# The scale and shift of two modulated norms as columns on transposed rows, in a two-block transformer kernel

## The chip, the cores and the metric

The kernel runs on one core of one Trainium2 chip as one program. The metric is device microseconds. The engines are TensorE (PE: matmuls and transposes into PSUM; PEld are its weight loads), VectorE (DVE), ScalarE (ACT) and GpSimd (POOL), with SyncE (SP) issuing most DMAs. Each engine works its own instructions in order and waits on semaphores for the others.

## The reference, cut to what matters

The input is x [1, 512, 2048] in float32. The first block is attention beside a state space mixer, an output projection and a LayerNorm. The second block modulates two RMS norms with six vectors from c:

```python
def rms_norm(x, g):
    return x * lax.rsqrt(jnp.mean(x * x, axis=-1, keepdims=True) + 1e-6) * g

h = first_block(x, ...)                  # ends in _layer_norm(ALPHA * h + mixed @ w_out, ln_g, ln_b)
shift1, scale1, gate1, shift2, scale2, gate2 = jnp.split(mod, 6, axis=-1)
u = rms_norm(h, norm1_g) * (1.0 + scale1) + shift1          # first modulated norm
u_a, v_a, q, k, v = jnp.split(u @ w_in, SPLIT_POINTS, axis=-1)
q, k = rms_norm(per head q, q_norm_g), rms_norm(per head k, k_norm_g)
y = concat(spatial_gating(u_a, v_a, gm_norm_g, gm_ws, gm_bs), stick_breaking_attention(q, k, v))
x = h + gate1 * (rms_norm(per group of 128 y, out_norm_g) @ w_out_2)
m = rms_norm(x, norm2_g) * (1.0 + scale2) + shift2          # second modulated norm
# top-1 of 4 expert groups, top-2 of its 8 experts (SwiGLU, 32 experts of width 256)
out = x + gate2 * moe(m)
```

## The kernel before, in words

Tokens lie in four tiles of 128 rows. A float32 product is made of three matmuls (L148 to L150) on a high and a low part of each operand. `wchunk` makes the parts of the weights: SP loads a raw chunk of 128x1024 (L136, four buffers), ACT casts the high part `wh` (L123, 1.05 us), DVE subtracts it for the low part `wl` (L124), three buffers each. `split_into` makes the two parts of an operand in the same lines, as pieces `op` of 128x256. PE's operands need the model dimension on the partitions, so rows are transposed by PE in blocks of four 128x128 tiles (L203) into a PSUM tile `s`.

*Norms* (`phase_b`, `norms`). The projection `w_out` runs for tokens 0 and 1 and then for 2 and 3. After each half, LayerNorm (L780, L781) and the first modulated norm follow token by token: DVE multiplies by the root `rs` and the broadcast row `g1` (L788), POOL adds the broadcast row `s1` (L789), and `rows_to_op` (L715) transposes and splits into `self.opt`. The four rows `lng`, `lnb`, `g1`, `s1` are 1 MB broadcasts that SP loads. While PE works at one half, DVE, POOL and ACT prepare the other.

*Mixer* (`mixer2`). The projections `w_in_2` read `self.opt`, again by halves for q and k. `head_norm` takes ACT squares of 128x128 (L798), a Newton root on DVE (L192 to L197) and a DVE multiply into a row tile (L803), which PE transposes. The mask multiply of the gating weights (`ws`, L854) is a DVE instruction there.

*Route* (`route`). `w_out_2` runs by halves. Per block of 512 columns DVE makes the residual `r` (L956, L957), POOL starts the second norm (L958: r times the row `gs`, which L926 and L927 make), ACT squares, PE transposes for the router's logits. After a half, ACT (L986) and POOL (L987), or DVE alone (L984), apply root and shift row `sh`, and ACT's queue writes `h2` to HBM (L988). DVE then works out the routing (L999 and on) with one ACT exponential (L1010). The router's own columns `col` are loaded element by element (L889 to L891).

*Gather and experts.* POOL's indirect DMAs fetch 8 tiles of 128 gathered rows of `h2` (L1136), PE transposes them in blocks, ACT (L1149, even blocks) and DVE (L1145, odd blocks) evacuate them into `xg`; for the first tile the other engine copies a window for expert 0 (L1147, L1151). 32 experts follow with 1 MB weight loads.

The order on each engine is fixed when the program is built, by a scheduler that follows the code's order and `issue_after` hints.

Of the kernel before, what the change touches and what calls it, by code (L numbers as in the profile page):

```python
# [103 lines left out]
class Kern:  # L104
# [622 lines left out]
    def phase_b(self):  # L727
# [3 lines left out]
        self.x1 = self.dram.tile([512, 2048], F32, name='x1')  # L731
        with tc.tile_pool(name='ln', **kw) as ln:
            t = [ln.tile([128, 2048], F32, name=n) for n in ('lng', 'lnb', 'g1', 's1')]
            lng, lnb, g1, s1 = t
            st = ln.tile([128, 4, 4, 6], F32, name='st')

            def load(k):

                if k < 2:
                    nc.sync.dma_start(r[:, k, :], a['x'][k])  # L740
                elif k < 6:
                    src = (a['norm1_g'], self.mod[:, 2048:4096], a['ln_g'], a['ln_b'])[k - 2]
                    nc.sync.dma_start((g1, s1, lng, lnb)[k - 2], src.broadcast_to([128, 2048]))
                    if k == 3:
                        nc.vector.scalar_tensor_tensor(g1, s1, 1.0, g1, OP.add, OP.mult)
                elif k == 6:
                    nc.sync.dma_start(s1, self.mod[:, 0:2048].broadcast_to([128, 2048]))
                else:
                    for i in (2, 3):
                        nc.sync.dma_start(r[:, i, :], a['x'][i])  # L750

            for half in ((0, 1), (2, 3)):
# [10 lines left out]
                for i in half:  # L763
                    self.norms(ln, i, st[:, i], lng, lnb, g1, s1)
        with tc.tile_pool(name='rt', **kw) as self.rt:
            with tc.tile_pool(name='b2', **kw) as b2:
                self.mixer2(b2, self.opt)
            with tc.tile_pool(name='m0', **kw) as self.m0:
                self.route()

    def norms(self, ln, i, st, lng, lnb, g1, s1):
# [14 lines left out]
        for b in range(4):  # L786
            c = slice(b * 512, b * 512 + 512)
            nc.vector.scalar_tensor_tensor(t[:, c], r[:, i, c], rs, g1[:, c], OP.mult, OP.mult)  # L788
            nc.gpsimd.tensor_tensor(t[:, c], t[:, c], s1[:, c], OP.add)  # L789
            self.rows_to_op(t[:, c], self.opt[2 * b:2 * b + 2], i)  # L790

    def head_norm(self, pool, x, g, out, scale=1.0 / 128, eps=1e-6):
# [8 lines left out]
        for h in range(4):  # L801
            c = slice(h * 128, h * 128 + 128)
            nc.vector.scalar_tensor_tensor(out[:, c], x[:, c], rs[:, h:h + 1], g[h], OP.mult, OP.mult)  # L803

    def mixer2(self, b2, op):
        tc, nc, a, r = self.tc, self.nc, self.a, self.r
        kw = dict(bufs=1, side='right', reuse_waits='tile')
        gq = self.row_bcast(b2, a['q_norm_g'], 128, 'gq')
        gk = self.row_bcast(b2, a['k_norm_g'], 128, 'gk')
# [16 lines left out]
        with tc.tile_pool(name='sb', **kw) as sb:  # L826
            for b, g, half in ((0, gq, (0, 1)), (1, gk, (0, 1)), (0, gq, (2, 3)), (1, gk, (2, 3))):
                ps = self.gemm('R', a['w_in_2'][b], op, bg=1, toks=half)
                xT = qk[b]
                for i in half:  # L830
                    t = b2.tile([128, 512], F32, tag='row', name='row', bufs=3)
                    self.head_norm(b2, ps[i], [g] * 4, t)
# [21 lines left out]
            nc.vector.tensor_tensor(ws, ws, self.mask_le[:, None, :].to_broadcast([128, 4, 128]), OP.mult)  # L854
            ps = self.gemm('R', a['w_in_2'][3], op)
            for i in range(4):
                t = b2.tile([128, 512], F32, tag='row', name='row', bufs=3)
                vn = b2.tile([128, 512], F32, tag='row', name='vn', bufs=3)
                nc.scalar.activation(t, ps[i], AF.Gelu)
                self.head_norm(b2, t, [gm[:, h * 128:(h + 1) * 128] for h in range(4)], vn)  # L860
# [10 lines left out]
            for i in range(4):  # L871
                t = b2.tile([128, 512], F32, tag='row', name='row', bufs=3)
                self.head_norm(b2, o[:, i, :], [go[:, 512 + h * 128:512 + (h + 1) * 128] for h in range(4)], t)
                self.rows_to_op(t, opy[0:2], i)
            for i in range(4):
                t = b2.tile([128, 512], F32, tag='row', name='row', bufs=3)
                vn = b2.tile([128, 512], F32, tag='row', name='vn', bufs=3)
                nc.scalar.activation(t, ps[i], AF.Gelu)  # L878
                nc.vector.tensor_tensor(t, t, sg[:, i, :], OP.mult)
                self.head_norm(b2, t, [go[:, h * 128:(h + 1) * 128] for h in range(4)], vn)  # L880
# [4 lines left out]
    def router(self):  # L885

        nc, a, xr = self.nc, self.a, self.rt
        col = xr.tile([128, 3, KT], F32, name='col')
# [16 lines left out]
    def route(self):  # L905
# [35 lines left out]
        for half in ((0, 1), (2, 3)):  # L941
# [5 lines left out]
            for b in range(4):  # L947
# [5 lines left out]
                for i in half:  # L953
# [4 lines left out]
                    nc.gpsimd.tensor_tensor(h2[i % 2][:, c], r[:, i, c], gs[:, c], OP.mult)  # L958
# [173 lines left out]
    def gather(self, s):  # L1132
# [319 lines left out]
```

## Time and profile before

| what | value |
|---|---|
| median of 3 runs | 2021.39 us (2020.11 to 2024.66) |
| profiled execution | 2020.36 us, span 2018.5 us, mean granted clock 0.973 |
| PE busy | 1909.2 us, 95% of the span |
| DVE, ACT, POOL busy | 1217.5, 862.8, 325.9 us |
| HBM traffic | 479.76 MB read, 37.84 MB written |

Times in the trace count from the start of the span. The first block's mixers run to about 838 us, the norms and `w_out` to 1070, the mixer of the second block to about 1330, route to 1445, the gather to 1500, the experts to the end. An idle time in brackets stands before the instruction that ended it, with what released it. The granted clock is that of TensorE, as a share of 2.4 GHz; 0.50 is the level of 1.2 GHz.

### The profile page before, as it was taken

How to read it: one execution, taken by the hardware profiler on the slowest of the kernel's cores; microseconds unless marked ns; L12 is line 12 of the kernel's file. 1: busy time of each engine (PE TensorE's matmuls, PEld its weight loads, DVE VectorE, ACT ScalarE, POOL GpSimd, SP SyncE). 2: the span in 40 equal slices, each digit the busy share in tenths (PEclk: the TensorE clock that was granted, in tenths of full speed). 3: DMA queues.
4: the chain of work that ended last, by engine and by line, in shares of the span. 5: the costliest groups of instructions: out<-in, count | busy, mean ns of one | idle time of the engine just before them, and what ended most of it. 6: DMA issues, size and time to landing. Idle time of an engine off the chain costs nothing. (4 is left out here: it accounts for less than half of the span.)

```text
span 2018.5 us, 30419 instructions
## 1 busy us (share of the span) xinstructions
PE 1909.2 (95%) x11830; PEld 1232.9 (61%) x11830; DVE 1217.5 (60%) x2210; ACT 862.8 (43%) x1426; POOL 325.9 (16%) x251
## 2 busy tenths in 40 slices
PE   8999999999999999999997999889589999999996
PEld 5677776666777778887876888778442333333331
DVE  4778975444677796558796664877633434333433
ACT  3343223335443453434444554644234444444453
POOL 0422133000011110001111120043331111111111
PEclk9999999999999999999998999989699999999998
DMA  8654664545665674586654332656699999999994
GB/s 305 224 188 166 232 230 169 181 179 204 239 218 199 213 258 136 183 311 235 197 200 144 116 116 96 248 199 219 260 346 358 399 400 399 401 403 396 401 416 183
DMA packets 115493, 502.85 MB, mean 249 GB/s; under 512 B 22299, under 2 KB 23835, under 8 KB 84499
## 3 DMA queue, kind: packets, MB, share of 16 engines
q1 hardware_dynamic: 108642, 479.81, 64.0%
q0 software_dynamic: 6080, 16.83, 3.2%
q10 hardware_dynamic: 624, 4.24, 0.5%
q8 instruction: 94, 1.54, 0.3%
q14 instruction: 53, 0.43, 0.1%
HBM read 479.76 MB, written 37.84 MB: 256 GB/s over the span
## 5 line engine op out<-in xcount | busy, mean ns | idle before, releaser
L124 DVE TENSOR_TENSOR wl<-raw,wh 128x1024 fp32r<-128x1024 f32 (+1 forms) x272 | 357.8, 1320 | 224.4 <-ACT wh L123 223.5
L123 ACT CAST wh<-raw 128x1024 fp32r<-128x1024 f32 (+1 forms) x272 | 280.5, 1031 | 445.9 <-PE g L150 200.7
L149 PE MATMUL g<-wl,op 128*128 128x512 f32 (+1 forms) x896 | 351.0, 392 | 5.6 <-DVE wl L124 5.5
L150 PE MATMUL g<-wh,op 128*128 128x512 f32 (+1 forms) x896 | 348.3, 389 | 0.0
L148 PE MATMUL g<-wh,op 128*128 128x512 f32 (+1 forms) x896 | 333.7, 393 | 2.1 <-ACT row L878 1.0
L148 PE MATMUL g<-op,wh 128*128 128x512 f32 x672 | 272.0, 406 | 4.4 <-ACT z L404 3.0
L149 PE MATMUL g<-op,wh 128*128 128x512 f32 x672 | 268.1, 400 | 0.0
L150 PE MATMUL g<-op,wl 128*128 128x512 f32 x672 | 262.2, 396 | 0.0
L1178 PE MATMUL s<-wop,x 128*32 128x512 f32 x1710 | 251.4, 593 | 0.0
L1180 PE MATMUL s<-wop,x 128*32 128x512 f32 x570 | 251.0, 593 | 0.0
L148 PEld LDWEIGHTS g<-wh,op 128*128 128x128 f32 x896 | 171.2, 191 | 42.8 <-issue 6.6
L149 PEld LDWEIGHTS g<-wl,op 128*128 128x128 f32 x896 | 171.0, 191 | 41.6 <-DVE wl L124 8.5
L150 PEld LDWEIGHTS g<-wh,op 128*128 128x128 f32 x896 | 170.8, 191 | 33.4 <-issue 1.1
L1178 PEld LDWEIGHTS s<-wop,x 128*32 128x32 f32 x1710 | 68.2, 110 | 158.2 <-issue 154.0
L148 PEld LDWEIGHTS g<-op,wh 128*128 128x128 f32 x672 | 127.6, 190 | 52.9 <-issue 19.7
L150 PEld LDWEIGHTS g<-op,wl 128*128 128x128 f32 x672 | 127.3, 189 | 31.6 <-issue 3.9
L1188 ACT COPY yt<-g 32x512 f32<-32x512 f32 x192 | 111.3, 580 | 79.4 <-DVE y L1271 43.2
L149 PEld LDWEIGHTS g<-op,wh 128*128 128x128 f32 x672 | 127.9, 190 | 26.2 <-issue 1.4
L1178 PE MATMUL g<-wop,hT 128*32 128x512 f32 x810 | 120.7, 592 | 3.7 <-ACT hT L1227 2.2
L1189 DVE TENSOR_TENSOR gu<-gu,s 96x512 f32<-96x512 f32 x32 | 21.8, 682 | 169.5 <-ACT gu L1188 169.5
L1188 ACT COPY gu<-s 32x512 f32<-32x512 f32 x96 | 55.6, 579 | 159.1 <-PE s L1180 157.5
L1180 PE MATMUL g<-wop,hT 128*32 128x512 f32 x270 | 120.9, 594 | 0.0
(400 smaller groups left out, 2817.9 us busy)
## 6 DMA issues: line engine op xcount, KB each, us to landing
wop<-in_w_gu SPq DMA_DIRECT2D x95, 1024.0 KB
raw<-in_w_in SPq DMA_DIRECT2D x168, 512.0 KB
wm<-in_w_mod SPq DMA_DIRECT2D x96, 512.0 KB
raw<-in_w_mod SPq DMA_DIRECT2D x96, 512.0 KB
raw<-in_w_out SPq DMA_DIRECT2D x96, 512.0 KB
wop<-in_w_dn SPq DMA_DIRECT2D x45, 1024.0 KB
w<-in_w_gu SPq DMA_DIRECT2D x33, 1024.0 KB
w<-in_w_dn SPq DMA_DIRECT2D x19, 1024.0 KB
```

The lines of the kernel that those rows point to most:

```text
L123: nc.scalar.copy(hi, src)
L124: (lo_eng or nc.vector).tensor_tensor(lo, src, hi.bitcast(F32), OP.subtract)
L148: nc.tensor.matmul(out, lhsT=a[0], rhs=b[0], start=start, stop=False)
L149: nc.tensor.matmul(out, lhsT=a[0], rhs=b[1], start=False, stop=False)
L150: nc.tensor.matmul(out, lhsT=a[1], rhs=b[0], start=False, stop=stop)
L1178: nc.tensor.matmul(main[i][32 * s:32 * s + 32], lhsT=xs[i][:, 32 * s:32 * s + 32], rhs=w[i], start=first[i], stop=last[i], tile_position=( ...
L1180: self.mm = nc.tensor.matmul(ps[o][96:128], lhsT=xs[3][:, 32 * o:32 * o + 32], rhs=w[3], start=first[3], stop=last[3], tile_position=(0, 96))
L1188: self.last_copy = nc.scalar.copy(t[32 * s:32 * s + 32], ps[s][96:128])
L1189: nc.vector.tensor_tensor(t, t, main[0:W], OP.add)
```

## The change

In `norms`, ACT scales a row block by the root alone (Copy, scale `rs`); PE transposes it; ACT applies scale and bias columns to each 128x128 tile of the transposed block (Identity, 16 per token) into an SBUF tile `f` of two buffers, and the operand pieces are split from `f`. The columns `n1col` are loaded element by element (128 partitions x 16). In `route`, the rows `sh` and `gs` and all POOL work on `h2` go; `h2` becomes the residual times the root, by ACT (8 instructions of 128x512 per half). Scale and shift of the second norm are applied behind the gather: every 128x128 tile of a block gets the router's columns `col2`, by ACT Identity or DVE tensor_scalar, 64 each, and the first windows are copied from `xg` afterwards. The columns `col2` now lie in a pool that is open earlier. A new pool `hn`, opened before the norms' pool, holds the head norms' gains `gq` and `gk`, their sums and row tiles (all `head_norm` calls take it), so these no longer lie in the space that the norms use. The mask multiply of `ws` is put behind the last head norm of q and k.

```diff
@@ -729,22 +729,25 @@
...
+        hn_cm = tc.tile_pool(name='hn', bufs=1)
+        self.hn = hn_cm.__enter__()
...
-            t = [ln.tile([128, 2048], F32, name=n) for n in ('lng', 'lnb', 'g1', 's1')]
-            lng, lnb, g1, s1 = t
+            lng, lnb = [ln.tile([128, 2048], F32, name=n) for n in ('lng', 'lnb')]
...
+            col = ln.tile([128, 3, KT], F32, name='n1col')
...
             def load(k):
...
                 if k < 2:
                     nc.sync.dma_start(r[:, k, :], a['x'][k])
-                elif k < 6:
-                    src = (a['norm1_g'], self.mod[:, 2048:4096], a['ln_g'], a['ln_b'])[k - 2]
-                    nc.sync.dma_start((g1, s1, lng, lnb)[k - 2], src.broadcast_to([128, 2048]))
+                elif k < 5:
+                    src = (a['norm1_g'], self.mod[:, 2048:4096], self.mod[:, 0:2048])[k - 2]
+                    nc.sync.dma_start(col[:, k - 2, :], src.rearrange('o (k p) -> p (o k)', p=128))
                     if k == 3:
-                        nc.vector.scalar_tensor_tensor(g1, s1, 1.0, g1, OP.add, OP.mult)
-                elif k == 6:
-                    nc.sync.dma_start(s1, self.mod[:, 0:2048].broadcast_to([128, 2048]))
+                        nc.vector.scalar_tensor_tensor(col[:, 0, :], col[:, 1, :], 1.0, col[:, 0, :], OP.add, OP.mult)
+                elif k < 7:
+                    nc.sync.dma_start((lng, lnb)[k - 5], (a['ln_g'], a['ln_b'])[k - 5].broadcast_to([128, 2048]))
@@ -785,9 +789,16 @@
...
         for b in range(4):
             c = slice(b * 512, b * 512 + 512)
-            nc.vector.scalar_tensor_tensor(t[:, c], r[:, i, c], rs, g1[:, c], OP.mult, OP.mult)
-            nc.gpsimd.tensor_tensor(t[:, c], t[:, c], s1[:, c], OP.add)
-            self.rows_to_op(t[:, c], self.opt[2 * b:2 * b + 2], i)
+            nc.scalar.activation(t[:, c], r[:, i, c], AF.Copy, scale=rs)
+            pt = self.sps()
+            self.transposes(pt, [t[:, (4 * b + j) * 128:(4 * b + j + 1) * 128] for j in range(4)])
+            f = ln.tile([128, 512], F32, tag='f', name='f', bufs=2)
+            for j in range(4):
+                k, cj = 4 * b + j, slice(j * 128, j * 128 + 128)
+                nc.scalar.activation(f[:, cj], pt[:, cj], AF.Identity, scale=g1[:, k:k + 1], bias=s1[:, k:k + 1])
+            for u in range(2):
+                o, ts = self.opt[2 * b + u], slice(i * 128, i * 128 + 128)
+                self.split_into(o[0][:, :, ts], o[1][:, :, ts], f[:, u * 256:(u + 1) * 256].rearrange('p (k t) -> p k t', k=2))
...
@@ -851,13 +862,14 @@
...
-            nc.vector.tensor_tensor(ws, ws, self.mask_le[:, None, :].to_broadcast([128, 4, 128]), OP.mult)
+            with tc.issue_after(self.last_hn.ins):
+                nc.vector.tensor_tensor(ws, ws, self.mask_le[:, None, :].to_broadcast([128, 4, 128]), OP.mult)
@@ -885,7 +897,7 @@
...
-        col = xr.tile([128, 3, KT], F32, name='col')
+        col = self.col2 = self.xr.tile([128, 3, KT], F32, name='col')
@@ -919,13 +931,7 @@
...
-        sh = m0.tile([128, 2048], F32, name='sh')
         h2 = [m0.tile([128, 2048], F32, name='h2_%d' % i) for i in range(2)]
-        gs = self.row_bcast(m0, a['norm2_g'], 2048, 'g2')
-        nc.sync.dma_start(sh, self.mod[:, 8192:10240].broadcast_to([128, 2048]))
-        nc.gpsimd.tensor_tensor(sh, sh, gs, OP.mult)
-        nc.gpsimd.tensor_tensor(gs, sh, gs, OP.add)
-        nc.sync.dma_start(sh, self.mod[:, 6144:8192].broadcast_to([128, 2048]))
@@ -955,7 +961,6 @@
...
                     nc.vector.tensor_tensor(r[:, i, c], r[:, i, c], t, OP.add)
-                    nc.gpsimd.tensor_tensor(h2[i % 2][:, c], r[:, i, c], gs[:, c], OP.mult)
                     nc.scalar.activation(t, r[:, i, c], AF.Square, accum_out=ss[:, i, b:b + 1])
@@ -978,13 +983,7 @@
             for i in half:
                 for b in range(4):
                     c = slice(b * 512, b * 512 + 512)
-                    t = h2[i % 2][:, c]
-                    rs = r2[:, i - half[0]:i - half[0] + 1]
-                    if b >= 2:
-                        nc.vector.scalar_tensor_tensor(t, t, rs, sh[:, c], OP.mult, OP.add)
-                    else:
-                        nc.scalar.activation(t, t, AF.Copy, scale=rs)
-                        nc.gpsimd.tensor_tensor(t, t, sh[:, c], OP.add)
+                    nc.scalar.activation(h2[i % 2][:, c], r[:, i, c], AF.Copy, scale=r2[:, i - half[0]:i - half[0] + 1])
@@ -1138,17 +1137,19 @@
...
             pt = self.gps() if b % 2 else self.sps()
             self.transposes(pt, [t[:, (4 * b + j) * 128:(4 * b + j + 1) * 128] for j in range(4)])
-            k4 = slice(4 * b, 4 * b + 4)
-            src = pt.rearrange('p (k t) -> p k t', k=4)
-            dst = self.xg[:, k4, s * 128:(s + 1) * 128]
-            if b % 2:
-                nc.vector.tensor_copy(dst, src)
-                if s == 0:
-                    nc.scalar.copy(self.spread(self.win[0][:, k4, :]), src[:, :, 0:W].rearrange('p k (b a) -> p k b a', a=16))
-            else:
-                nc.scalar.copy(dst, src)
-                if s == 0:
-                    nc.vector.tensor_copy(self.spread(self.win[0][:, k4, :]), src[:, :, 0:W].rearrange('p k (b a) -> p k b a', a=16))
+            for j in range(4):
+                k = 4 * b + j
+                g, sh = self.col2[:, 0, k:k + 1], self.col2[:, 2, k:k + 1]
+                src, dst = pt[:, j * 128:j * 128 + 128], self.xg[:, k, s * 128:(s + 1) * 128]
+                if b % 2:
+                    nc.vector.tensor_scalar(dst, src, g, sh, OP.mult, OP.add)
+                else:
+                    nc.scalar.activation(dst, src, AF.Identity, scale=g, bias=sh)
+            if s == 0:
+                k4 = slice(4 * b, 4 * b + 4)
+                (nc.scalar.copy if b % 2 else nc.vector.tensor_copy)(
+                    self.spread(self.win[0][:, k4, :]), self.xg[:, k4, 0:W].rearrange('p k (b a) -> p k b a', a=16))
```

ACT around the norms of tokens 2 and 3, before (`hn_jk` are the head norms' squares, `op` operand pieces, `wh` weight casts):

```order
L123 CAST wh<-raw 128x1024 x5
L123 CAST op<-s 128x2x128 x4
L798 ACTIVATE hn_jk,hn_ss<-g 128x128 x3
L123 CAST op<-s 128x2x128
L798 ACTIVATE hn_jk,hn_ss<-g 128x128
L123 CAST op<-s 128x2x128
L798 ACTIVATE hn_jk,hn_ss<-g 128x128
L123 CAST op<-s 128x2x128
L798 ACTIVATE hn_jk,hn_ss<-g 128x128
L123 CAST op<-s 128x2x128
L798 ACTIVATE hn_jk,hn_ss<-g 128x128 x8
L835 COPY r<-s 128x4x128
```

and now, a stretch of the same place, with `f` the scaled and shifted blocks:

```order
L123 CAST wh<-raw 128x1024
L798 ACTIVATE f<-s,n1col 128x128 x4
L123 CAST wh<-raw 128x1024
L123 CAST op<-f 128x2x128 x4
L123 CAST wh<-raw 128x1024
L809 ACTIVATE hn_jk,hn_ss<-g 128x128
L798 ACTIVATE f<-s,n1col 128x128 x4
L123 CAST wh<-raw 128x1024
L809 ACTIVATE hn_jk,hn_ss<-g 128x128
L798 ACTIVATE f<-s,n1col 128x128 x4
L123 CAST op<-f 128x2x128 x2
L809 ACTIVATE hn_jk,hn_ss<-g 128x128
```

Squares of the head norms, Identity instructions, pieces and weight casts now alternate, where the squares stood behind the norms' pieces.

DVE at the head norms, before: the mask multiply L854 in the midst of two heads' roots, ahead of the first row (L803):

```order
L197 SCALAR_TENSOR_TENSOR rs_y<-rs_t,rs_y 128x4 x2
L195 TENSOR_TENSOR rs_t<-rs_y 128x4 x2
L196 SCALAR_TENSOR_TENSOR rs_t<-rs_t,hn_ss 128x4
L854 TENSOR_TENSOR ws<-ws,cst 128x512
L196 SCALAR_TENSOR_TENSOR rs_t<-rs_t,hn_ss 128x4
L197 SCALAR_TENSOR_TENSOR rs_y<-rs_t,rs_y 128x4 x2
L195 TENSOR_TENSOR rs_t<-rs_y 128x4
L803 SCALAR_TENSOR_TENSOR row<-g,rs_y,gq 128x128 x4
```

and now, at the last of the rows for q and k (L814; the first stands 110 rows earlier):

```order
L814 SCALAR_TENSOR_TENSOR row<-g,rs_y,gk 128x128 x4
L196 SCALAR_TENSOR_TENSOR rs_t<-rs_t,hn_ss 128x4
L197 SCALAR_TENSOR_TENSOR rs_y<-rs_t,rs_y 128x4
L195 TENSOR_TENSOR rs_t<-rs_y 128x4
L196 SCALAR_TENSOR_TENSOR rs_t<-rs_t,hn_ss 128x4
L197 SCALAR_TENSOR_TENSOR rs_y<-rs_t,rs_y 128x4
L814 SCALAR_TENSOR_TENSOR row<-g,rs_y,gk 128x128 x4
L866 TENSOR_TENSOR ws<-ws,cst 128x512
L57 TENSOR_SCALAR z<-s 128x512
```

The mask multiply (L866) moved from ahead of the first row to behind the last; L57 is the attention's first step.

ACT from the first gathered tile to the end of the evacuations, before (`gu`, `h`: the first expert):

```order
L1149 COPY xg<-s 128x4x128 x2
L1147 COPY x_11804<-g 128x4x6x16
L1149 COPY xg<-s 128x4x128
L1147 COPY x_11804<-g 128x4x6x16
L1149 COPY xg<-s 128x4x128 x4
L1188 COPY gu<-s 32x512 x3
L1149 COPY xg<-s 128x4x128 x2
L1221 ACT_TABLE_LOAD
L1221 ACTIVATE h<-gu 96x256
L1149 COPY xg<-s 128x4x128 x7
```

and now, counted in 128x128 tiles, four to a block:

```order
L1148 ACTIVATE xg<-s,col 128x128 x8
L1151 COPY x_11840<-xg 128x4x6x16
L1148 ACTIVATE xg<-s,col 128x128 x4
L1151 COPY x_11840<-xg 128x4x6x16
L1148 ACTIVATE xg<-s,col 128x128 x12
L1189 COPY gu<-s 32x512 x3
L1148 ACTIVATE xg<-s,col 128x128 x4
L1222 ACT_TABLE_LOAD
L1222 ACTIVATE h<-gu 96x256
L1148 ACTIVATE xg<-s,col 128x128 x36
```

Seven block copies behind the first expert's activation became 36 tile instructions, nine blocks, and only one block instead of two stands between `gu` and the table load.

## Rows read from the trace of the kernel before

**Rows 1.** The page, part 1: each engine's busy time, share of the span, instructions.

```profile
PE 1909.2 (95%) x11830; PEld 1232.9 (61%) x11830; DVE 1217.5 (60%) x2210; ACT 862.8 (43%) x1426; POOL 325.9 (16%) x251
```

**Rows 2.** Windows: each engine's busy us (instructions), then PEclk, DMA share, GB/s.

```profile
838.00:1070.00 232.00, 220.45 (x982) 180.72 (x981) 180.06 (x269) 99.70 (x129) 31.13 (x16) 0.99 0.66 236
1078.10:1083.70 5.60, 5.60 (x15) 4.41 (x16) 4.22 (x32) 2.71 (x15) 0.00 (x0) 0.50 0.57 56
1350.00:1360.00 10.00, 8.38 (x35) 7.53 (x36) 9.32 (x7) 2.41 (x6) 9.92 (x6) 0.67 0.57 208
1445.00:1500.00 55.00, 37.16 (x302) 23.14 (x306) 22.49 (x74) 16.68 (x25) 21.98 (x22) 0.78 0.84 313
1560.00:1990.00 430.00, 430.00 (x3946) 131.50 (x3942) 165.14 (x269) 203.31 (x324) 69.97 (x53) 1.00 1.01 401
```

**Rows 3.** Waits of PE, 838 to 1500 us: waited for, us in total, times, longest.

```profile
PE s L203 <- DVE row L803: 11.8, 1, 11.8
PE s L1038 <- DVE small L1033: 11.6, 1, 11.6
...
PE s L203 <- POOL t L789: 6.6, 4, 2.6
PE g L149 <- DVE wl L124: 5.5, 5, 2.5
```

**Rows 4.** Timeline of PE: start, us, work, [idle before it <- releaser].

```profile
955.15 0.66 PE L203 MATMUL s<-cst,t 128*128 128x128 f32 x4 [2.28 <-POOL t L789]
...
1065.62 0.66 PE L203 MATMUL s<-cst,t 128*128 128x128 f32 x4 [1.44 <-POOL t L789]
...
1078.09 1.16 PE L203 MATMUL s<-cst,row 128*128 128x128 f32 x4 [11.81 <-DVE row L803]
...
1351.62 0.50 PE L149 MATMUL g<-wl,op 128*128 128x512 f32 x1 [2.50 <-DVE wl L124]
...
1488.33 1.12 PE L203 MATMUL s<-cst,y 128*128 128x128 f32 x4 [1.79 <-ACT xg L1149]
```

**Rows 5.** Timeline of DVE around the first head norm of the second block.

```profile
1076.59 0.69 DVE L854 TENSOR_TENSOR ws<-ws,cst 128x512 f32<-128x512 f32 x1 [4.06 <-DMA ws<-in_gm_ws]
```

**Rows 6.** Timeline of ACT: one weight cast in the steady gemm before it.

```profile
1024.65 1.06 ACT L123 CAST wh<-raw 128x1024 fp32r<-128x1024 f32 x1 [1.67 <-PE g L150]
```

**Rows 7.** By line: operation, count, duration in ns min/median/max, starts, shapes.

```profile
L530 ACT ACTIVATE cacc<-cu,vec_a x16: 802/816/836, 531.1 to 748.9; 128x512 f32<-128x512 f32 x16
...
L798 ACT ACTIVATE hn_jk<-g x32: 277/278/301, 1066.6 to 1129.8; 128x128 f32<-128x128 f32 x32
...
L1149 ACT COPY xg<-s x16: 563/586/649, 1459.4 to 1493.8; 128x512 f32<-128x512 f32 x16
...
L867 DVE TENSOR_SCALAR r<-s,bs x16: 340/343/351, 1252.8 to 1279.0; 128x128 f32<-128x128 f32 x16
```

**Rows 8.** Timeline of SP's queue: element by element loads of the router's columns.

```profile
1072.11 5.49 SPq L890 DMA_DIRECT2D col<-mod  x1
```

**Rows 9.** Timeline of POOL in the route stage.

```profile
1340.38 4.60 POOL L926 TENSOR_TENSOR sh<-sh,g 128x2048 f32<-128x2048 f32 x1 [111.47 <-PE g L150]
...
1350.56 11.22 POOL L958 TENSOR_TENSOR h<-r,g 128x512 f32<-128x512 f32 x6
```

**Rows 10.** Timeline of DVE in the route stage.

```profile
1341.49 12.31 DVE L124 TENSOR_TENSOR wl<-raw,wh 128x1024 fp32r<-128x1024 f32 x3 [4.37 <-ACT wh L123]
...
1357.09 2.30 DVE L124 TENSOR_TENSOR wl<-raw,wh 128x1024 fp32r<-128x1024 f32 x1
```

**Rows 11.** Timeline of DVE at the end of route.

```profile
1434.09 5.77 DVE L984 SCALAR_TENSOR_TENSOR h<-h,rs_y,sh 128x512 f32<-128x512 f32 x4
```

**Rows 12.** Timeline of ACT at the end of route.

```profile
1432.24 2.56 ACT L986 ACTIVATE h<-h,rs_y 128x512 f32<-128x512 f32 x4 [0.50 <-DVE rs_y L197]
...
1436.97 1.28 ACT L1010 ACT_TABLE_LOAD   x1 [2.17 <-DVE h L984]
1440.26 0.22 ACT L1010 ACTIVATE small<-small 128x16 f32<-128x16 f32 x1 [2.01 <-DVE small L1009]
```

More of the change, by code (lines that the diff above doesn't have):

```diff
@@ L763, in phase_b @@
                 for i in half:
-                    self.norms(ln, i, st[:, i], lng, lnb, g1, s1)
+                    self.norms(ln, i, st[:, i], lng, lnb, col[:, 0, :], col[:, 2, :])
         with tc.tile_pool(name='rt', **kw) as self.rt:
@@ L767, in phase_b @@
                 self.mixer2(b2, self.opt)
+            hn_cm.__exit__(None, None, None)
             with tc.tile_pool(name='m0', **kw) as self.m0:
@@ L802, in head_norm @@
             c = slice(h * 128, h * 128 + 128)
-            nc.vector.scalar_tensor_tensor(out[:, c], x[:, c], rs[:, h:h + 1], g[h], OP.mult, OP.mult)
+            self.last_hn = nc.vector.scalar_tensor_tensor(out[:, c], x[:, c], rs[:, h:h + 1], g[h], OP.mult, OP.mult)
     def mixer2(self, b2, op):
@@ L807, in mixer2 @@
         kw = dict(bufs=1, side='right', reuse_waits='tile')
-        gq = self.row_bcast(b2, a['q_norm_g'], 128, 'gq')
-        gk = self.row_bcast(b2, a['k_norm_g'], 128, 'gk')
+        gq = self.row_bcast(self.hn, a['q_norm_g'], 128, 'gq')
+        gk = self.row_bcast(self.hn, a['k_norm_g'], 128, 'gk')
         bs = b2.tile([128, 4], F32, name='bs')
@@ L830, in mixer2 @@
                 for i in half:
-                    t = b2.tile([128, 512], F32, tag='row', name='row', bufs=3)
-                    self.head_norm(b2, ps[i], [g] * 4, t)
+                    t = self.hn.tile([128, 512], F32, tag='row', name='row', bufs=3)
+                    self.head_norm(self.hn, ps[i], [g] * 4, t)
                     pt = self.sps()
@@ L852, in mixer2 @@
                 nc.sync.dma_start(self.gate1[b], self.mod[:, 4096 + b * 512:4608 + b * 512].broadcast_to([128, 512]))
-            nc.vector.tensor_tensor(ws, ws, self.mask_le[:, None, :].to_broadcast([128, 4, 128]), OP.mult)
+            with tc.issue_after(self.last_hn.ins):
+                nc.vector.tensor_tensor(ws, ws, self.mask_le[:, None, :].to_broadcast([128, 4, 128]), OP.mult)
             ps = self.gemm('R', a['w_in_2'][3], op)
             for i in range(4):
-                t = b2.tile([128, 512], F32, tag='row', name='row', bufs=3)
-                vn = b2.tile([128, 512], F32, tag='row', name='vn', bufs=3)
+                t = self.hn.tile([128, 512], F32, tag='row', name='row', bufs=3)
+                vn = self.hn.tile([128, 512], F32, tag='row', name='vn', bufs=3)
                 nc.scalar.activation(t, ps[i], AF.Gelu)
-                self.head_norm(b2, t, [gm[:, h * 128:(h + 1) * 128] for h in range(4)], vn)
+                self.head_norm(self.hn, t, [gm[:, h * 128:(h + 1) * 128] for h in range(4)], vn)
                 pt = self.sps()
@@ L871, in mixer2 @@
             for i in range(4):
-                t = b2.tile([128, 512], F32, tag='row', name='row', bufs=3)
-                self.head_norm(b2, o[:, i, :], [go[:, 512 + h * 128:512 + (h + 1) * 128] for h in range(4)], t)
+                t = self.hn.tile([128, 512], F32, tag='row', name='row', bufs=3)
+                self.head_norm(self.hn, o[:, i, :], [go[:, 512 + h * 128:512 + (h + 1) * 128] for h in range(4)], t)
                 self.rows_to_op(t, opy[0:2], i)
             for i in range(4):
-                t = b2.tile([128, 512], F32, tag='row', name='row', bufs=3)
-                vn = b2.tile([128, 512], F32, tag='row', name='vn', bufs=3)
+                t = self.hn.tile([128, 512], F32, tag='row', name='row', bufs=3)
+                vn = self.hn.tile([128, 512], F32, tag='row', name='vn', bufs=3)
                 nc.scalar.activation(t, ps[i], AF.Gelu)
                 nc.vector.tensor_tensor(t, t, sg[:, i, :], OP.mult)
-                self.head_norm(b2, t, [go[:, h * 128:(h + 1) * 128] for h in range(4)], vn)
+                self.head_norm(self.hn, t, [go[:, h * 128:(h + 1) * 128] for h in range(4)], vn)
                 self.rows_to_op(vn, opy[2:4], i)
```

## The prediction

> **What bounds the kernel now.** I read the page's busy line first: PE is busy 95% of the span [rows 1], so the time is PE's chain of work plus its idle, and a change that adds no PE work can win or lose only in idle and in clock. The windows by stage come next. The expert phase, 1560 to 1990 us, has PE busy all 430 us and the DMA engines at a share of 1.01 [rows 2]: nothing is late there, so what is won before 1500 us reaches the end and what is lost is not caught up. In the three stages that the change touches PE idles: 232.00 - 220.45 = 11.6 us between 838 and 1070, and 55 - 37.2 = 17.8 us between 1445 and 1500 [rows 2]. The list of PE's waits names the releasers [rows 3], and the timeline places them [rows 4]. The page's chain of waits covers only the last two microseconds and is not used.
>
> **The change part by part**, against the profiled execution's own 2020.4 us (span 2018.5), 1.0 us under the median of 2021.4.
>
> *One price first.* The new work is 128 ACT Identity instructions of 128x128 (64 in the norms, 64 after the gather), each with a scale and a bias column, where 32 blocks were evacuated or split whole before. No row shows that shape. A 128x128 Square takes 278 ns, a 128x512 Identity with two columns 816, a plain 128x512 copy 586 [rows 7]. From 278 to 586 over 384 columns the slope is 0.80 ns a column, so 816 - 384 x 0.80 = 509 ns alone; the four of a block follow each other some 0.1 us closer, as the 2.56 us for four of 707 ns, thus 0.64 apiece, suggest [rows 12]. I take 0.41 us apiece, 1.65 a block; the ends are 0.28 and 0.82. The Trainium skill (ScalarE: Activation LUTs, What ACT_TABLE_LOAD costs) gives an ACTIVATE 186 ns, 0.833 ns a column, 93 ns for each column operand, and 93 ns of overlap. That estimate is 0.39 apiece, which no run here has shown; by it the sum would be about 1 us better, and my second rival, which needs 0.6, would be unlikely.
>
> *First half's norms (tokens 0, 1).* DVE's multiply and POOL's add go, and with them a PE wait of 2.28 us [rows 4], one of the four on POOL that make 6.6 us [rows 3]. ACT gets 8 scalings (0.64) and 32 Identity: 5.1 + 13.1 = 18.2 us, beside the 16 operand casts it did already. In the steady gemm ACT idles 1.67 us per weight chunk [rows 6], and these instructions are spread over ten chunks: 16.7 us of room, plus a lead of about 3 us because there are three weight buffers and PE's own transposes. Nearly full, so I expect about 1 us of new waits for weights and count +1; ends +2.3 (all hidden) and -3.
>
> *Second half and the first head norms.* PE's 11.81 us before the first head row [rows 4] is two things. First, the last operand pieces are late, since the DVE and POOL passes of token 3 run one after the other. Second, DVE then works on the head norm's reciprocal root, and the mask multiply, put in the middle of it, makes it wait 4.06 us for the ws load [rows 5], which SP issues only once the norm's pool is free. The change moves the mask multiply behind the last head norm and loads the head norms' gains early; the order then shows the head rows of tokens 0 and 1 worked off between the norms of tokens 2 and 3. What is late next is ACT: squares, scalings, 32 Identity, operand casts and weight casts in one order. Following that order at the durations above, the operand pieces of token 3's first block are ready near 1065 us, so PE starts the second-half gemm at about 1065.5 where it now starts at 1079, after an idle of about 5.5 us. That is 13.5 us. PE ran its first 5.6 us after the gap at a granted clock of 0.50, its 1.2 GHz level [rows 2], which cost 2.8 us; a gap of 5.5 us will probably cost that again. I take 3.5 off for weight casts queued behind squares and Identity instructions: +10. Ends: +16.3 (no gap, no half clock) and 0, the gap as long as before.
>
> *Route.* Three 1 MB broadcasts, POOL's L926 and L927 and its 24 small passes go. Beside them three weight subtractions of DVE took 12.31 us, against 2.30 for one later [rows 10], while POOL ran 4.60 us and then almost without pause to 1361 [rows 9]. PE waited 5.5 us for DVE's weights in five waits, one of 2.50 [rows 3, 4]; the 1350 to 1360 stretch had a granted clock of 0.67 [rows 2], 0.33 x 8.38 = 2.8 us. ACT instead scales both tokens whole: 8 instructions in a row, 5 us, where four took 2.56 [rows 12], which may hold a weight cast back by 1 to 2 us. Not all five waits lie in this stage, so I take 5.1 of the 5.5: 5.1 + 2.8 - 2.4 = +5.5. Ends +8.3 and +2.
>
> *End of route.* DVE's 5.77 us of scale and shift [rows 11] stand ahead of the routing. They go, but the routing then needs ACT's exponential: it starts at 1440.26 now [rows 12], and in the new order behind eight scalings and the table load, 1432.24 + 5.1 + 1.3 = 1438.6. So 1.6 us, not 5.8: I take +1.5; ends 0 and +4, since both h2 writes are now issued behind the exponential and the gathers read them.
>
> *Gather, 1458 to 1500.* Each of 16 ACT blocks goes from 0.59 to 1.65 us; DVE's from one copy to four of 0.34 that overlap [rows 7], about 1.1. Early blocks lie beside expert matmuls. In the last stretch PE already waits for ACT's evacuation (1.79 us at 1488.33 [rows 4]), and the order puts nine ACT blocks behind the first expert's activation: 14.9 us from about 1486, ending near 1501 where the last now starts at 1493.8 [rows 7] and ends 0.6 later. The copies for the next expert read these blocks, first those of the first half of the columns, so PE loses some 5, and 1 more at the first tile, where the copy now waits for the evacuation: -6. Ends 0 and -14.
>
> *Column loads.* Six loads of 2048 single elements. Such a load held SP's queue for 5.49 us [rows 8], and weight loads stand behind it. The router's three move to the first weight loads of w_out, the other three replace two broadcasts in the first half. DVE's product of two of these columns waits for the last of them, and weight subtractions are queued behind it, for which PE waits; it waited for the broadcasts in the same place. Raw weights are four deep: -1; ends 0 and -5. The Trainium skill (DMA: Bandwidth & Descriptors, Rules for kernel authors) says that a non-contiguous last dimension becomes one descriptor per element and should be avoided. Its rule would have all three hold the queue as long, 16 us, and PE lose the -5; the row beside it bears that out for one load.
>
> Sum: 1 + 10 + 5.5 + 1.5 - 6 - 1 = 11. 2020.4 - 11 = 2009.4, and on the level of the median 2010.4: I forecast 2010.
>
> **The rivals.**
> 1. *ACT is the new bound before it is in the norms as well* (gain about 5, 2016). The weight cast stands in ACT's order behind runs of six or eight Identity instructions that themselves wait for PE's transposes; 18 us into 17 us of room speaks for it, the lead of three buffers against it. First half -2 instead of +1, second +7 instead of +10: 11 - 3 - 3 = 5, with the median's 1.0 2016.
> 2. *Slower: the small ACT instruction costs 0.6 us.* One mechanism, a fixed cost per instruction of two column operands, in 24 instructions ahead of PE's restart, 32 in the first half and 40 in the gather's end. Each 0.1 us costs 2.4 + about 3 + 4 = 9.4 us, so the gain of 11 is gone at 0.53 us, and at 0.6 the time is 2020.4 + 17.9 - 11, with the median's 1.0 about 2028. For: no row has the shape, and the 128x512 form is at 816 ns. Against: the slope above.
> 3. *More comes through* (2002). Second half +13, first +2, end of route +3, gather -3, the rest as above: 19.5. The gather's early blocks lie beside expert matmuls, which speaks for it; the one ACT queue speaks against it.
> 4. *The wait only changes its name*: the second-half gap stays because operand pieces, not the ws load, set it. The second half then gives 2 instead of 10, 2018. The 4.06 us in the head norm speak against it.
>
> **How the numbers follow.** Forecast 0.50, first rival 0.17, second 0.13, third 0.14, fourth 0.06. A difference under 0.2%, 4 us, can't be told from none here. Faster by more (under 2017.3): the forecast 0.47 of its 0.50, the first rival 0.14 of its 0.17, the third all, the fourth 0.02: 0.77. Slower (over 2025.4): the second rival's 0.11, and 0.02 of the others: 0.13. Within: 0.10. The forecast's own range is 2003 to 2018; with the third rival's 2002 and half of the second the range is 1998 to 2026.
>
> **What would show it.** PE's wait for POOL gone, and the wait before the first head row replaced by one of 4 to 7 us for operand pieces near 1060; no stretch of half clock at 1350; Identity 128x128 at about 0.5 us, four in 1.65; ACT nearly without pause from 1486 to 1501 and the next expert's start about 6 us after the gather's present length, measured from the routing's end. Wrong if the gather stage grows by more than 12 us, if PE's waits for weights between 930 and 1070 exceed 8 us, or if PE's second-half gemm starts no earlier than now.

## The result, and the profile after

The changed kernel takes 1998.78 us at the median of 6 runs (1990.91 to 2002.47), the kernel before 2020.86 beside it; the ratio is 0.9893, interval 0.9872 to 0.9914. Forecast was 2010, range 1998 to 2026: faster as forecast, but by 22 us where the sum said 11, and 0.8 us above the lower end of the range. The profiled execution has a span of 1998.3 us. Its busy line, the windows (columns as in [rows 2]) and PE's waits (as in [rows 3]):

```profile
PE 1904.1 (95%) x11830; PEld 1224.5 (61%) x11830; DVE 1174.1 (59%) x2234; ACT 910.5 (46%) x1562; POOL 241.4 (12%) x209
```
```profile
838.00:1070.00 232.00, 230.54 (x1049) 189.70 (x1047) 162.68 (x298) 135.69 (x227) 0.00 (x0) 1.00 0.66 227
1030.00:1070.00 40.00, 39.53 (x195) 32.45 (x194) 31.68 (x108) 39.04 (x98) 0.00 (x0) 1.00 0.58 200
1429.00:1475.00 46.00, 37.20 (x240) 21.36 (x244) 24.80 (x73) 29.96 (x73) 15.85 (x17) 0.80 0.90 311
1540.00:1970.00 430.00, 430.00 (x3950) 131.48 (x3944) 164.90 (x269) 202.63 (x323) 69.72 (x53) 1.00 1.01 401
```
```profile
PE s L203 <- DMA y<-h,tok: 11.2, 1, 11.2
PE s L1037 <- DVE small L1032: 7.2, 1, 7.2
...
PE s L1179 <- DVE x L1202: 4.0, 1, 4.0
PE s L203 <- ACT xg L1148: 3.9, 4, 1.9
...
PE g L149 <- DVE wl L124: 1.5, 3, 0.7
```

PE idles 1.5 us between 838 and 1070 where it idled 11.6 [rows 2]; the waits for POOL and for the head row are gone. The table gives the stages of each profiled execution, worked out from PE's timeline: first w_out matmul, first attention matmul (`r`), first transpose of route, first routing matmul, first gathered transpose, first matmul of expert 1, end of the span.

| profile | first block | norms, q, k | mixer | route | to gather | gather | experts | span |
|---|---|---|---|---|---|---|---|---|
| before | 828.3 | 310.1 | 200.9 | 106.0 | 12.9 | 36.9 | 523.4 | 2018.5 |
| changed | 832.1 | 286.1 | 202.7 | 91.6 | 16.5 | 43.3 | 525.9 | 1998.3 |
| e1 | 828.6 | 299.9 | 200.5 | 108.4 | 13.0 | 37.1 | 524.7 | 2012.2 |
| e2 | 827.3 | 304.3 | 200.5 | 105.3 | 12.8 | 37.0 | 524.5 | 2011.7 |
| e3 | 832.5 | 309.8 | 200.4 | 92.3 | 16.5 | 41.8 | 524.7 | 2018.0 |
| e4 | 832.2 | 288.4 | 200.0 | 104.7 | 12.6 | 36.4 | 525.7 | 2000.1 |
| e5 | 831.9 | 307.7 | 202.5 | 100.9 | 12.7 | 29.3 | 524.1 | 2009.1 |
| e6 | 830.3 | 285.6 | 202.9 | 96.8 | 16.8 | 40.8 | 525.5 | 1998.7 |
| e7 | 828.6 | 293.1 | 198.2 | 92.3 | 16.5 | 39.9 | 526.9 | 1995.5 |
| e8 | 823.9 | 286.6 | 201.0 | 91.6 | 14.6 | 39.9 | 525.5 | 1983.1 |
| e9 | 831.6 | 287.6 | 201.0 | 91.6 | 16.7 | 43.2 | 524.8 | 1996.6 |
| e10 | 831.2 | 286.7 | 201.0 | 91.6 | 16.3 | 41.8 | 528.1 | 1996.7 |
| e11 | 831.8 | 287.2 | 200.0 | 91.6 | 14.6 | 41.7 | 526.4 | 1993.2 |
| e12 | 830.8 | 286.8 | 202.5 | 100.6 | 13.4 | 34.9 | 521.3 | 1990.2 |

The first block, whose code no kernel changes, takes 823.9 to 832.5 us, so a total differs by a few microseconds for no reason in the edit; stages and ratios carry the verdicts. A stage is that of one execution, though, and differs where its code is the same: the norms by 2.8 us with the first norm and the pool changed (285.6 to 288.4, without e7), the route by 7.8 with the old second norm (100.6 to 108.4) and 0.7 with the new (91.6 to 92.3, without e6), the gather by 7.8 with the old (29.3 to 37.1) and 3.4 with the new (39.9 to 43.3). The experiments ran on three chips, e1 to e4, e5 to e8 and e9 to e12; the kernel before takes 2020.98, 2015.59 and 2022.11 us beside them, so ratios are compared, not times. Against before: norms -24.0, route -14.4, the way to the gather +3.6, gather +6.4, experts +2.5, +3.8 in the first block and +1.8 in the mixer, where little but the head norms' pool differs.

The restart of PE in the second half, first in PE's timeline (columns as in [rows 4]), then in ACT's:

```profile
1058.61 0.60 PE L203 MATMUL s<-cst,t 128*128 128x128 f32 x4
1058.97 0.48 PE L148 MATMUL g<-wh,op 128*128 128x512 f32 x1
...
1061.80 0.60 PE L203 MATMUL s<-cst,row 128*128 128x128 f32 x4
...
1063.63 0.60 PE L203 MATMUL s<-cst,row 128*128 128x128 f32 x4
```
```profile
1058.24 1.58 ACT L798 ACTIVATE f<-s,n1col 128x128 f32<-128x128 f32 x4
...
1060.81 1.61 ACT L798 ACTIVATE f<-s,n1col 128x128 f32<-128x128 f32 x4
1062.17 0.84 ACT L123 CAST op<-f 128x256 fp32r<-128x256 f32 x2
```

The last transposes of token 3's norm run at 1058.61, and nothing follows but work: PE starts the second-half gemm with token 2 at 1058.97, where it started near 1079 before. The first pieces of token 3 are cast by 1063.0, close to the 1065 forecast, but the order puts 18 matmuls of token 2 (six for each of three weight chunks, about 4.1 us) and two head rows in front of token 3's first matmul, which comes behind the row at 1063.63. So the pieces were late for nobody.

The new instructions by line, and the end of the gather on ACT:

```profile
L798 ACT ACTIVATE f<-s,n1col x64: 440/492/678, 957.5 to 1067.5; 128x128 f32<-128x128 f32 x64
...
L1148 ACT ACTIVATE xg<-s,col x64: 438/462/624, 1430.3 to 1472.2; 128x128 f32<-128x128 f32 x64
...
L1146 DVE TENSOR_SCALAR xg<-g,col x64: 396/401/410, 1431.1 to 1467.6; 128x128 f32<-128x128 f32 x64
```
```profile
1462.92 9.87 ACT L1148 ACTIVATE xg<-s,col 128x128 f32<-128x128 f32 x28 [1.48 <-PE g L203]
1472.87 3.02 ACT L1202 COPY x<-xg 128x768 f32 x2
```

One Identity lasts 492 and 462 ns (medians), and in a row they follow each other by 9.87/28 = 0.35 us; 0.41 was taken. ACT ends its blocks at 1472.8 without a pause, and PE stands still before expert 1, for which DVE copies the rows. DVE begins that copy after 3.49 us without work, while ACT is at its last blocks; the profile names no releaser ("issue"), and e10 tests whether ACT's blocks are it. PE's timeline, then DVE's:

```profile
1459.56 0.66 PE L203 MATMUL s<-cst,y 128*128 128x128 f32 x4 [1.94 <-ACT xg L1148]
...
1472.40 1.07 PE L1179 MATMUL s<-w,x 128*32 128x512 f32 x3 [4.01 <-DVE x L1202]
```
```profile
1471.49 1.57 DVE L1202 COPY x<-xg 128x768 f32 x2 [3.49 <-issue]
```

From the routing to the gather, on DVE, POOL and SP's queue:

```profile
1411.11 0.17 DVE L1010 TENSOR_REDUCE small<-small 128x4 f32<-128x16 f32 x1 [1.10 <-ACT small L1009]
...
1417.91 0.17 DVE L1074 CAST tok<-s 128x8 int32<-128x8 f32 x1 [0.63 <-PE s L1071]
1421.40 0.24 DVE L1297 TENSOR_SCALAR past<-stc,cst 96x32 f32<-96x32 f32 x1 [3.32 <-DMA out<-r]
```
```profile
1422.61 1.29 POOL L1135 DMA_INDIRECT y<-h,tok  x1 [213.92 <-DVE tab L1100]
```
```profile
1399.77 0.33 SPq L1291 DMA_DIRECT2D gate<-mod  x1
1400.15 0.43 SPq L974 DMA_DIRECT2D out<-r  x1
1400.67 1.33 SPq L1169 DMA_DIRECT2D w<-in_w_gu  x2
1402.05 0.77 SPq L974 DMA_DIRECT2D out<-r  x1
1402.87 0.67 SPq L1169 DMA_DIRECT2D w<-in_w_gu  x1
```

The token list is ready at 1418.1, but DVE's next instruction waits 3.32 us for the write of `out`, and the first gather goes out at 1422.61, 4.5 us behind the list; before it was 0.9 us (1450.81 to 1451.73), and PE's wait for the gathered rows was 7.6 us, not 11.2. The gather's releaser in the profile, a `tab` instruction, is none that the gather reads from, so whether the write of `out` or that of `h2` held POOL isn't shown. SP's queue had sent out's second half between loads of 1 MB.

### The profile page after: what moved, and what is told of

It is laid out like the page before. It is cut to its first block, busy times and chain, and to the rows that moved or that the text cites. A ratio compares the mean times of both kernels' runs of the same rounds, so it can differ in the third digit from the quotient of the medians.

```text
span 1998.3 us, 30489 instructions
## 1 busy us (share of the span) xinstructions
PE 1904.1 (95%) x11830; PEld 1224.5 (61%) x11830; DVE 1174.1 (59%) x2234; ACT 910.5 (46%) x1562; POOL 241.4 (12%) x209
## 5 line engine op out<-in xcount | busy, mean ns | idle before, releaser
L124 DVE TENSOR_TENSOR wl<-raw,wh 128x1024 fp32r<-128x1024 f32 (+1 forms) x272 | 335.7, 1237 | 223.6 <-ACT wh L123 221.2
```

The lines of the kernel that those rows point to most:

```text
L124: (lo_eng or nc.vector).tensor_tensor(lo, src, hi.bitcast(F32), OP.subtract)
```

## The experiments

**e1: the first norm's columns alone** (ratio 0.9957, 0.9941 to 0.9973).

Against the kernel before; `load` and the rest of `norms` as in the change, the head norms' tiles still in `b2`:

```diff
-            nc.vector.scalar_tensor_tensor(t[:, c], r[:, i, c], rs, g1[:, c], OP.mult, OP.mult)
-            nc.gpsimd.tensor_tensor(t[:, c], t[:, c], s1[:, c], OP.add)
-            self.rows_to_op(t[:, c], self.opt[2 * b:2 * b + 2], i)
+            nc.scalar.activation(t[:, c], r[:, i, c], AF.Copy, scale=rs)
...
```

> Only the first modulated norm is changed (scale and shift as columns on transposed rows); the head norms' tiles stay in the mixer's pool, the mask multiply stays where it was, the second norm is as before. Theory 1 (the second half's 22 us need the head norms' own pool, because squares and rows of tokens 0 and 1 can only then be worked off between the norms): the PE wait before the first head row stays at 5 us or more, the second half gains 5 to 12 us, the run is 2007 to 2014 us. Theory 2 (the 22 us come from the norms' shorter chain, without POOL and with half of DVE's work): the wait falls under 2 us and the run is near 1996. Both: first half about 3 us faster.

```profile
PE s L203 <- DVE row L811: 12.5, 1, 12.5
```

```profile
1068.84 1.16 PE L203 MATMUL s<-cst,row 128*128 128x128 f32 x4 [12.54 <-DVE row L811]
```

PE's waits in the norms, and its timeline. POOL's waits are gone, and the one before the head row is as long as before; but the row comes 240.3 us into the stage (1068.84 - 828.56), where it came after 249.8 (1078.09 [rows 4]). So the shorter chain doesn't shorten that wait, it only lets PE wait earlier, and the stage wins 10.2 us.

**e2: the head norms' pool and the late mask alone** (0.9970, 0.9954 to 0.9987).

```diff
+        hn_cm = tc.tile_pool(name='hn', bufs=1)
...
-        gq = self.row_bcast(b2, a['q_norm_g'], 128, 'gq')
+        gq = self.row_bcast(self.hn, a['q_norm_g'], 128, 'gq')
...
+            with tc.issue_after(self.last_hn.ins):
```

> Only the pool of the head norms and the later mask multiply; both modulated norms are as before. Theory 1 (pool needed and nearly enough): the wait of 11.8 us before the first head row goes, a wait for operand pieces or for POOL of 2 to 6 us stays, the run is 2005 to 2012 us. Theory 2 (the chain of the norms sets the gap): PE still waits 8 us or more before the second-half gemm, the run is 2015 to 2021.

```profile
PE s L203 <- POOL t L792: 5.9, 3, 2.6
...
PE s L203 <- DVE row L806: 2.4, 1, 2.4
```

The head row's wait falls to 2.4 us, as theory 1 has it, POOL's waits stay, and the stage wins 5.8 us; the median of 2015.49 lies in theory 2's range. e1 and e2 add to 16.0, both together (e4) give 21.7 and the changed kernel 24.0. So neither part is enough alone: e1 leaves the head row's wait, e2 leaves POOL's. Some of what the two give only together is probably clock: over the stage the mean granted clock is 0.97 before, 0.98 in e1 and in e2, 1.00 in e4. An estimate from these: 0.01 of about 300 us is 3 us.

**e3: the second norm alone** (0.9997, 0.9982 to 1.0012). Router, route and gather of the changed kernel in the kernel before.

```diff
-                    nc.gpsimd.tensor_tensor(h2[i % 2][:, c], r[:, i, c], gs[:, c], OP.mult)
...
+                    nc.vector.tensor_scalar(dst, src, g, sh, OP.mult, OP.add)
```

> Only the second norm is changed (no rows of shift and scale in route, no POOL work there, columns behind the gather). Theory 1 (the route's 7 us come from POOL holding up DVE): PE's waits for weights in route go, its 0.67 clock at the start of route too, route is 6 to 8 us shorter; the gather is 6 us longer and the experts up to 3 us longer, so the run is within 2016 to 2021. Theory 2 (the route's gain in the changed kernel came from earlier work being done sooner): route is under 3 us shorter and the run is slower than before, 2022 to 2027.

Route -13.7, to the gather +3.5, gather +4.9: no difference in time that can be measured.

**e4: the first norm and the pool, the second norm as before** (0.9885, 0.9864 to 0.9906). Against the changed kernel:

```diff
+                    nc.gpsimd.tensor_tensor(h2[i % 2][:, c], r[:, i, c], gs[:, c], OP.mult)
...
-                    nc.vector.tensor_scalar(dst, src, g, sh, OP.mult, OP.add)
```

> The first norm's columns with the head norms' pool, and the second norm as before: the changed kernel without its second-norm part. If the parts add up by stage: first half 3 and second half 22 us faster, route and gather as before, so 1994 to 1999 us, no slower than the changed kernel. If the second norm's part was a real gain at the end: 2001 to 2005.

All of the changed kernel's gain is there without the second norm's part; its median is 1997.94.

**e5: the mask multiply alone** (0.9984, 0.9969 to 0.9998).

```diff
+            with tc.issue_after(self.last_hn.ins):
```

> The kernel before with the mask multiply of ws behind the last head norm and nothing else. If the load of ws that DVE waits for in the midst of the head norm sets the restart of PE: the 11.8 us wait shrinks by about 4 us and the run is near 2016. If it is only the last of several, with the pool of the head norms' tiles and the late norms behind it: the wait shrinks by 0 to 2 us, 2018 to 2021.

```profile
PE s L203 <- DVE row L803: 7.9, 2, 7.1
PE s L203 <- POOL t L789: 6.6, 4, 2.6
```

The longest head row wait falls from 11.8 to 7.1, the 4 us that DVE stood for ws [rows 5]; the stage wins 2.4. Of the other 7 us of the wait the pool takes 4.7, since e2, with both, leaves 2.4.

**e6: POOL's work put back into scratch** (0.9925, 0.9904 to 0.9946). Against the changed kernel; two of the three broadcasts, L926, L927 and 16 of the 24 small passes come back.

```diff
+                    nc.gpsimd.tensor_tensor(sh[:, c], r[:, i, c], gs[:, c], OP.mult)
```

> The changed kernel with POOL's work of the route stage put back into scratch rows: two 128x2048 passes and 16 of 128x512, whose result nobody reads, and two of the three broadcasts. If POOL held up DVE's weight subtractions (theory 1): DVE's weight subtractions at the start of route take 3 to 4 us each again, PE waits 3 us or more for weights there and route is 4 to 7 us longer than in the changed kernel. If DVE's own removed passes and the end's shorter chain were the gain (theory 2): under 2 us longer.

```profile
1319.88 10.81 DVE L124 TENSOR_TENSOR wl<-raw,wh 128x1024 fp32r<-128x1024 f32 x3 [3.72 <-ACT wh L123]
```
```profile
1317.22 4.62 POOL L938 TENSOR_TENSOR sh<-sh,g 128x2048 f32<-128x2048 f32 x1 [110.81 <-DMA sh<-mod]
1321.91 5.44 POOL L939 TENSOR_TENSOR g<-sh,g 128x2048 f32<-128x2048 f32 x1
```

DVE's and POOL's timelines at the start of route: three weight subtractions take 10.81 us beside POOL, as in [rows 9, 10], where one takes 1.23 us in the changed kernel, and route grows by 5.2 us. PE waits 1.9 us for weights, less than the 3 expected, 1.7 for the residual `r`, and 1.5 more for the routing. Theory 1 holds for that much of the 14.4; as a time e6 isn't told apart from the changed kernel. The rest is seen in the route's windows (columns as in [rows 2]) before, in e5, in e6 and changed:

```profile
1339.29:1445.30 106.01, 88.59 (x459) 75.40 (x458) 78.08 (x109) 45.29 (x72) 51.41 (x26) 0.89 0.58 214
```
```profile
1342.12:1442.99 100.87, 82.72 (x457) 70.22 (x455) 77.44 (x109) 45.16 (x72) 50.73 (x26) 0.94 0.62 222
```
```profile
1318.83:1415.62 96.79, 83.02 (x457) 70.04 (x455) 65.47 (x101) 50.06 (x80) 36.65 (x18) 0.96 0.55 193
```
```profile
1320.93:1412.57 91.64, 82.79 (x457) 70.83 (x455) 50.66 (x101) 50.22 (x80) 0.00 (x0) 0.95 0.57 199
```

Before, PE is busy 88.6 us at a mean clock of 0.89, in e6 83.0 at 0.96: 5.6 of the other 9 us. In it lies the slow stretch behind PE's wait of 2.5 us [rows 4], with a clock of 0.88 and 0.70 in the two 8 us from 1347.3 on, where e5, e6 and the changed kernel have 1.00 that far into the stage. PE's wait for the routing, 11.6 [rows 3] against 8.7, gives 2.9. But e5 and e12 have the old second norm too, no wait over 1.3 us for weights and no such stretch, and their routes are 100.9 and 100.6. So some 5 of the 14.4 us come and go without the edit; 9 are left of it against these two.

**e7: 32 Identity more in the norms** (0.9913, 0.9890 to 0.9936).

```diff
+                if j % 2:
+                    nc.scalar.activation(f[:, cj], pt[:, cj], AF.Identity, ...)
```

> The changed kernel with every second Identity of the norms issued twice: 32 more 128x128 instructions on ACT, about 11 us of ACT work in all, the same result. If ACT is at its limit there (it is busy 39.0 of 40 us between 1030 and 1070): PE waits 4 to 6 us more in the second half and 0 to 3 in the first, the run is 4 to 9 us slower than the changed kernel. If ACT still has room: under 2 us.

```profile
PE g L148 <- ACT op L123: 4.0, 1, 4.0
```

PE waits 4.0 us for an operand piece and the stage is 7.0 us longer than in the changed kernel, for about 11 us of ACT work: ACT was within some 4 us of being the bound. As a time e7 isn't told apart from the changed kernel.

**e8: 4 MB of loads behind the h2 writes** (0.9881, 0.9857 to 0.9906). The loads go to ACT's queue, so they no longer stand ahead of the writes of `out` either.

```diff
-                nc.sync.dma_start(self.gate2, ...)
+                with tc.issue_after(self.h2_write.ins):
+                    nc.scalar.dma_start(self.gate2, ...)
...
+        q = self.nc.scalar if self.loads < 3 else self.nc.sync
```

> The changed kernel with the load of gate2 and the first three weight loads of expert 1 (4 MB) issued behind the h2 writes, on ACT's queue, and not ahead of them on SP's. If the first gather waits for the writes of h2 and out that share the DMA engines with these 4 MB: the first gather is issued 3.5 to 4.7 us earlier after the routing's end, PE's wait of 11.2 us for the gathered rows falls to 7 or 8, and the run is 2 to 4 us faster than the changed kernel. If the expert phase is then held by the loads that came later, nothing is left of it at the end.

```profile
1409.48 1.29 POOL L1135 DMA_INDIRECT y<-h,tok  x1 [208.49 <-DVE tab L1100]
```
```profile
PE s L203 <- DMA y<-h,tok: 9.3, 1, 9.3
```

First gather and PE's wait for it: the gather goes out 6.4 us behind the routing's first matmul (1403.1), not 10.0 (1422.61 - 1412.57), and PE waits 9.3 instead of 11.2. PE's wait was expected at 7 or 8. The loads now fall on the gathers (DMA share 1.00 from the routing's first matmul to the first gathered transpose, 0.55 before and 0.90 changed), so of the 3.6 us 2.0 come back and 1.6 stay. As a time it is not told apart from the changed kernel.

**e9 to e12, one chip.** e9 is the changed kernel again (0.9875, 0.9853 to 0.9897). e10 (0.9858, 0.9837 to 0.9878) and e11, with e8's edit too (0.9850, 0.9826 to 0.9875):

```diff
-                if b % 2:
+                if b % 2 or (s >= 6 and b == 2):
```

e12 is e4 with e8's edit (0.9847, 0.9830 to 0.9865).

> The changed kernel once more, beside the next three on one chip, as their measure. A ratio to the kernel before of 0.987 to 0.992 is expected, and the unchanged first stage (to the start of w_out) anywhere between 823 and 833 us, as it was in the profiles so far.

> The changed kernel, in which DVE and not ACT scales and shifts the third block of the last two gathered tiles: 8 of ACT's 64 instructions less. If ACT's instructions in one queue set the gather's end (they ran without pause for 9.87 us up to 1472.8 in the changed kernel): the copies for expert 1 start 2 to 3 us earlier and the run is 1 to 3 us faster than the changed kernel. If PE's half clock and the gathers' landing set it: the same within 1 us.

```profile
1460.17 7.10 ACT L1148 ACTIVATE xg<-s,col 128x128 f32<-128x128 f32 x20 [1.46 <-remote]
1467.90 3.02 ACT L1202 COPY x<-xg 128x768 f32 x2 [0.64 <-DVE xg L1146]
```
```profile
1465.16 2.63 DVE L1146 TENSOR_SCALAR xg<-s,col 128x128 f32<-128x128 f32 x8
1467.71 1.57 DVE L1202 COPY x<-xg 128x768 f32 x2
```

ACT's last run is 2.8 us shorter, the gather only 1.4: DVE's copy no longer waits for ACT, but it comes behind DVE's own eight tiles. In this profile the experts are 3.3 us longer than in e9, so its span shows no gain; as a time e10 isn't told apart from e9.

> The edit of e8 (the loads of 4 MB behind the h2 writes) and that of e10 together. If both hold: 3 to 7 us faster than the changed kernel. If the experts' loads take it back, 2 us or less.

> The second norm as before, the first norm and the pool as changed, and the 4 MB of loads behind the h2 writes as in e8. If the second norm's columns give away at the gather what they gain in route: within 3 us of e4's ratio 0.9885 or better, 0.986 to 0.989, and no slower than e11. If e11 is clearly faster, the second norm's columns pay once the loads are out of their way.

```profile
PE s L1050 <- DVE small L1045: 12.9, 1, 12.9
PE s L203 <- DMA y<-h,tok: 8.1, 1, 8.1
```

PE's waits in e12: 12.9 for the routing (11.6 before), but 8.1 for the gather (7.6 before, 11.2 changed). Medians are 1998.77 (e9), 1994.95, 1992.44 and 1992.06: e12, with the second norm as before, is at least level with e11. Both are some 6 us below the changed kernel, with intervals that overlap.

## Why the prediction came out as it did

The sum was 11 us, the profile shows 20.2: 13 more in the norms and 4 more in route and the way to the gather, less 8 in the first block, the mixer and the experts, where nothing was forecast.

- *First half and second half, +11 forecast.* 24.0 measured, 22.5 in e9: 2.7 up to the end of w_out, by PE's timeline (forecast +1), 21.3 behind it (forecast +10, upper end 16.3). Of the two causes named for the 11.81 us the load of ws is shown (4.7 less in e5); the shorter chain of token 3 brings the row 9.5 us earlier, but PE as well, so that the wait stays at 12.5 (e1), and it took the head norms' pool to bring it to 2.4 (e2). The step that failed is "the operand pieces of token 3's first block are ready near 1065 us, so PE starts the second-half gemm at about 1065.5". The pieces' time was right; that PE must wait for them was not, since token 2's matmuls stood ahead and began at 1058.97. No idle, so no half clock either, and of the 3.5 us taken off for weight casts only waits of 0.36 and 0.53 us near 1070 are seen.
- *Identity price.* 0.35 in place of 0.41; the second rival (0.6) fell. The estimate of 0.39 by the Trainium skill (ScalarE: Activation LUTs, What ACT_TABLE_LOAD costs) was nearer than mine, and the estimate of 0.479 for one alone, by the same figures, lies between the 0.462 and 0.492 measured. By the second rival's 9.4 us for each 0.1 us, a price of 0.39 was worth 2 us, not the 1 said.
- *First rival, ACT as the bound.* Wrong here by little: ACT is busy 39.04 of 40 us, and e7 turned it into waits.
- *Third and fourth rival.* The third's 2002 is near the 1998.78 measured, but its second half of +13 was too small as well, and its gather of -3 didn't come. The fourth fell: no wait before the head row is left.
- *Route, +5.5, and its end, +1.5.* POOL's share as forecast (5.2 in e6), the clock as well, with the range that e5 gives; PE's wait for a weight cast behind the eight scalings, 2.4 in the sum, isn't seen. The 2.30 us that the sum set beside 12.31 was itself taken beside POOL; one subtraction takes 1.23 alone. The routing came earlier than the exponential allowed for, as DVE had other work ahead of it and waited only 1.10 us; but the gathers went out late and took 3.6 back. Net 10.8 where 7 stood, of which some 5 are in doubt.
- *Gather, -6.* 6.4 measured; with the spread of this stage that is agreement, not a proof of the size. The queue of ACT named is part of it, 1.4 us in e10 for 2.8 us less of ACT work.
- *Experts.* "What is won before 1500 us reaches the end" holds to 2 or 3 us: e10 lost its gain there. Why is left open.
- *Column loads, -1.* The chain is as told, the price smaller: DVE waits 5.12 us for the columns, three weight subtractions stand behind, and PE waits 0.25 us for them (1.24 in e4). The row of 5.49 us [rows 8] was the longest of three; the router's other two loads held the queue for 0.77 and 0.96 us.

```profile
867.24 0.17 DVE L748 SCALAR_TENSOR_TENSOR n1col<-n1col 128x16 f32<-128x16 f32 x1 [5.12 <-DMA n1col<-mod]
```

## What to carry to other kernels

When an engine waits for two things in turn, removing either alone lets it arrive earlier at the other, and the two edits together can win more than their parts (10.2 and 5.8 alone, 21.7 together, of one profile each). Before pricing a late operand, read from the order what the waiting engine has left to do that doesn't need it. Moving scale and shift behind a transpose multiplies instructions: here the route's gain was lost again on the way to the gather and in it, and e4, without that part, is as fast as the changed kernel.

## What was not expected

The gathers went out 3.6 us late because the writes ahead of them were queued with 1 MB weight loads: e8, which moves the loads, has the first gather at 6.4 us behind the routing again. DVE's wait of 3.32 us names the write of `out`, whose source rows lie where later tiles go. The gather stage itself moved without an edit. In before, then in e5 (columns as in [rows 2]):

```profile
1458.24:1495.14 36.90, 31.04 (x224) 20.50 (x225) 13.47 (x24) 13.66 (x23) 16.13 (x17) 0.85 0.93 358
```
```profile
1455.67:1484.98 29.31, 28.34 (x225) 18.38 (x225) 13.38 (x24) 13.30 (x23) 13.20 (x15) 0.94 1.01 372
```

In e5 the stage is 7.6 us shorter, at a clock of 0.94 against 0.85: PE's work is 2.7 us shorter and its idle 4.9. Why is open; e5 ran on another chip. So one profile of this stage can differ by as much as the edit.
